# The sample group's HGRN step: v spread over the partitions by TensorE, state loaded on GpSimd's queue, each head placed behind the prompt's own

## The chip, the cores and the metric

The kernel runs on one core of one Trainium2 chip. The metric is the device time of one execution in microseconds, of which the median over several runs is given.

## What is computed

The kernel is one step of a one-layer decoder with two groups of heads: attention heads and four HGRN2 heads of width 128. It runs for a prompt of 1024 tokens and for 8 samples of one token each, with the same weights. The change touches the HGRN2 heads of the 8 samples. Each sample b and head h has a state S of 128 key rows by 128 value columns, loaded from `state_hgrn`. With one token the reference's step is (cut from `_hgrn_chunk` and `_hgrn_inputs`):

```python
f = lb + (1.0 - lb) * sigmoid(z['f_b'])
k = (1.0 - lb) * sigmoid(-z['f_b'])
q = silu(z['q_b'])
v = z['i_b']
S_new = f[:, None] * S + k[:, None] * v[None, :]
o = q @ S_new
```

`f`, `k` and `q` are one number for each key row, `v` is one for each value column. `S_new` is an output (`hgrn_state_sample`), and `o` goes on, normalised, into the layer's output. The prompt's HGRN heads do the same over 1024 tokens, in chunks.

## The kernel before

`project()` (L280) normalises x, multiplies it by the wide input weight and runs the HGRN heads. The projections are float32 products made of three single-pass products (`xhi`/`xlo` by `w_hi`/`w_lo`, accumulated in `pa`); `feat` makes columns of features, `tok` rows of tokens. Each weight block is loaded by SP (`w_raw<-w_in`), then split by ScalarE (`w_hi`) and VectorE (`w_lo`). These weight matmuls are most of TensorE's work in this part and fill the time in which the HGRN heads wait for other engines.

The prompt heads are `hgrn_a(h)` (within-chunk sums `AT`, on all engines) and `hgrn_b(h)` (the running state `S` and the output `O`). At the end of `hgrn_b`, VectorE makes the norm `o_rs`, GpSimd scales `O` by it (L605), TensorE transposes `O` in two halves (`pt<-ident,O`, L609), ScalarE copies each half to `ot` (one buffer) and SP stores it to `oT_d`.

The sample heads are the generator `hgrn_sample()` (L419); each step from one `yield` to the next does one head. `v` is in `vs`, 8 partitions by 512. Before, it is written to a DRAM tile `v_d` once; each head loads it back to all 128 partitions as `vb` (L436, 512 KB) and loads its state `S` (L434, 512 KB), both on SP. VectorE multiplies `vb` by `k` (L438), GpSimd multiplies `S` by `f` (L439), VectorE adds them (L440), SP stores the sum. Then the sum is split into `S0h` (ScalarE) and `S0l` (VectorE), and 16 small products with `qp` make `o` in the PSUM tile `pt`.

Buffers are shared by tag in the pool `hp`, two of each tag: `S0` with the prompt state `S`, `vb` with `O`, `S0h`/`S0l` with the forget gates `F`. PSUM has one buffer for `pt`, two for `ph`, three for `pa`.

The code's order is not the program's: a list scheduler orders the instructions of each engine by its own estimate of durations. An engine then runs its instructions strictly in that order. `go(n)` in `project()` advances the sample generator and so says where in the code a sample head stands. Before, heads 0 and 1 stand between `hgrn_a(3)` and `hgrn_b(3)`, head 2 and 3 behind that.

Of the kernel before, what the change touches and what calls it, by code (L numbers as in the profile page):

```python
# [7 lines left out]
F32 = mybir.dt.float32  # L8
# [5 lines left out]
OP = mybir.AluOpType  # L14
# [6 lines left out]
NB = 8  # L21
# [6 lines left out]
class Kernel:  # L28
# [251 lines left out]
    def project(self, ctx):  # L280
        nc, a = self.nc, self.a
# [36 lines left out]
        def ev_q(h0):  # L318
            def ev(f, ts, p):
                h = h0 + f  # L320
                if ts.start == 0:
                    Q[h] = hp.tile([128, TS], F32, name="Q")
                nc.scalar.activation(Q[h][:, ts], p, AF.Sigmoid)
                nc.vector.tensor_tensor(Q[h][:, ts], p, Q[h][:, ts], op=OP.mult)
            return ev
# [10 lines left out]
        self.page_index(self.cp)  # L336
        smp = self.hgrn_sample()
        next(smp)
        for h in range(2):
            self.hgrn_b(h, *st[h])  # L340
        self.feat((C_FB + 256, 2, ev_f(2)))
        self.feat((C_QB + 256, 2, ev_q(2)))
        go = lambda n: [next(smp, None) for _ in range(n)]
        for h in range(2, 4):
            st = self.hgrn_a(h, Q[h], K[h], F[h])
            go(2 if h == 3 else 0)
            self.hgrn_b(h, *st)
            go(1 if h == 3 else 0)

        def ev_z(dst, scale):  # L350
            def ev(f, ts, p):
# [67 lines left out]
    def hgrn_sample(self):  # L419

        nc, hp, a = self.nc, self.hp, self.a
        f, k, q = (self.sfkq[:, i] for i in range(3))
        v_d = self.dram.tile([NB, 512], F32, name="v_d")
        self.after(self.pidma, nc.sync.dma_start(v_d, self.vs))
        o = hp.tile([32, 128], F32, name="so", bufs=1)
        for h in range(4):
            yield
            po = self.ps_t.tile([128, 512], F32, name="pt")[:64, :128]
            qp = hp.tile([128, NB, 64], F32R, name="qp", bufs=1)
            nc.vector.tensor_scalar(qp.rearrange("p (a c) d -> p a (c d)", c=2), self.ones[:, None, :].to_broadcast([128, 4, 128]), 0.0, None, op0=OP.mult)  # L430
            qv = qp.rearrange("p b c -> p (b c)")
            self.split(qv[:, h * NB:h * NB + 456:65], qv[:, 32 + h * NB:32 + h * NB + 456:65], q[:, h], nc.vector, nc.vector)
            S = hp.tile([128, NB, 128], F32, name="S0", tag="S")
            nc.sync.dma_start(S, a["state_hgrn"][0, :, h].rearrange("b k v -> k b v"))  # L434
            vb = hp.tile([128, NB, 128], F32, name="vb", tag="O")
            nc.sync.dma_start(vb, bass.AP(tensor=v_d.tensor, offset=v_d.offset + h * 128, ap=[[0, 128], [512, NB], [1, 128]]))  # L436
            bc = lambda t: t[:, h, :, None].to_broadcast([128, NB, 128])
            nc.vector.tensor_tensor(vb, vb, bc(k), op=OP.mult)  # L438
            nc.gpsimd.tensor_tensor(S, S, bc(f), op=OP.mult)  # L439
            nc.vector.tensor_tensor(S, S, vb, op=OP.add)  # L440
            nc.sync.dma_start(a["hgrn_state_sample"][0, :, h].rearrange("b k v -> k b v"), S)
            hi = hp.tile([128, NB, 128], F32R, name="S0h", tag="F")
            lo = hp.tile([128, NB, 128], F32R, name="S0l", tag="F")
            self.split(hi, lo, S, nc.scalar, nc.vector)
            for b in range(NB):
                self.mm(po, qp[:, b], hi[:, b], b == 0, False)
                self.mm(po[:32], qp[:, b, :32], lo[:, b], False, b == NB - 1)
            if h:
                nc.vector.tensor_tensor(o, o, po[:32], op=OP.add)
            else:  # L450
                nc.vector.tensor_copy(o, po[:32])
            nc.vector.tensor_tensor(o, o, po[32:], op=OP.add)
        sq = hp.tile([32, 128], F32, name="ssq", bufs=1)
        ss = hp.tile([128, 1], F32, name="sr", bufs=1)[:32]
        nc.scalar.activation(sq, o, AF.Square, accum_out=ss)
        nc.vector.tensor_scalar(ss, ss, 1.0 / 128, EPS, op0=OP.mult, op1=OP.add)
        r = hp.tile([128, 1], F32, name="srs", bufs=1)[:32]
        self.rsqrt(hp, r, ss)
        nc.vector.tensor_scalar(o, o, r, None, op0=OP.mult)
        pt = self.ps_t.tile([128, 512], F32, name="pt")[:, :32]  # L460
        nc.tensor.transpose(pt, o, self.ident[:32, :32])
        oT = hp.tile([128, 32], F32, name="soT", bufs=1)
        nc.scalar.copy(oT, pt)
        nc.scalar.dma_start(self.oT_d[:, :, T:].rearrange("h v b -> v h b"), oT.rearrange("p (h b) -> p h b", b=NB))
# [177 lines left out]
    def page_index(self, pool):  # L642

        nc = self.nc
        pt = self.a["page_table"]
        raw = pool.tile([128, NB], I32, name="pt_raw", bufs=1)
        for i in range(8):
            dma = nc.sync.dma_start(raw[16 * i:16 * i + 16], bass.AP(tensor=pt.tensor, offset=pt.offset + i, ap=[[0, 16], [8, NB]]))
            if i == 0:
                self.pidma = dma  # L650
        lane = pool.tile([128, NB], I32, name="pt_lane", bufs=1)
        nc.gpsimd.iota(lane, pattern=[[0, NB]], base=0, channel_multiplier=1)
        nc.vector.tensor_scalar(lane, lane, 15, None, op0=OP.bitwise_and)
# [740 lines left out]
```

## Time and profile before

| | us |
|---|---|
| median of 3 runs | 1093.54 |
| lowest and highest | 1088.66, 1094.07 |
| the profiled execution | 1092.95 |
| its span in the trace | 1091.2 |
| TensorE busy (96%) | 1051.9 |
| VectorE busy (57%) | 618.0 |
| ScalarE busy (36%) | 388.5 |
| GpSimd busy (22%) | 241.1 |

The mean granted clock of TensorE is 0.984 of full speed. PE is TensorE, DVE VectorE, ACT ScalarE, POOL GpSimd; SP issues most DMAs. "Busy" of TensorE counts overlapping matmuls once, and a busy TensorE is not one at its peak. In a timeline the bracket behind a row tells how long its engine had been idle and what ended that. The HGRN part lies between about 80 and 390 us of the span, the sample heads between 282 and 376 us.

### The profile page before, as it was taken

Reading aid. Unit: us, or ns where it says so; the run is one execution under the profiler, and the core shown is the slowest. Engines: PE = TensorE matmul, PEld = TensorE weight load, DVE = VectorE, ACT = ScalarE, POOL = GpSimd, SP = SyncE. Lnnn points to the kernel's source line nnn. Section 1 sums busy time; section 2 is a strip of 40 time slices with the busy share of each in tenths; the row PEclk is TensorE's granted clock in tenths of the full one; section 3 lists DMA queues with packets and bytes.
Section 4 is the critical chain, followed back from the end, with each engine's and each line's share of the span. In section 5 each row is a group of like instructions: output and inputs, shape, how many; then the busy total and the mean of one; then the engine's idle time right before and its main releaser. Section 6 shows DMA issues by size and latency. Waiting matters only on the chain.

```text
span 1091.2 us, 18921 instructions
## 1 busy us (share of the span) xinstructions
PE 1051.9 (96%) x7021; PEld 936.8 (86%) x7021; DVE 618.0 (57%) x1822; ACT 388.5 (36%) x786; POOL 241.1 (22%) x276
## 2 busy tenths in 40 slices
PE   4999999999899899999989999999999999999998
PEld 3898799999789899999968898888788888778876
DVE  6847565666484535543574666766655677461223
ACT  4622234313133335432224544553554332241112
POOL 0024231331031133002023111111323133131111
PEclk9999999999999999999969999999999999999999
DMA  6212023333454666304468711001831474131110
GB/s 195 78 29 68 11 72 100 117 101 120 144 173 135 193 222 208 135 1 118 123 186 250 189 38 42 20 21 41 230 111 42 137 199 119 41 97 49 47 37 31
DMA packets 119007, 116.44 MB, mean 107 GB/s; under 512 B 18902, under 2 KB 101166, under 8 KB 116612
## 3 DMA queue, kind: packets, MB, share of 16 engines
q1 hardware_dynamic: 97412, 79.46, 25.6%
q10 hardware_dynamic: 19200, 19.01, 5.1%
q0 software_dynamic: 2304, 16.78, 4.6%
q8 instruction: 55, 0.90, 0.4%
q14 instruction: 36, 0.29, 0.1%
HBM read 84.84 MB, written 29.31 MB: 105 GB/s over the span
## 4 chain that ended last, share of the span: by engine, by line
PE 81%; DMA 9%; DVE 5%; issue 2%; ACT 1%; POOL 1%; SPq 0%; ACTq 0%; DVEq 0%; POOLq 0%
PE pa L42 37%; PE pb L42 27%; PE ph L42 9%; PE pt L42 4%; DMA vb<-v_d 2%; DMA w_raw<-w_in 2%; PE ph L714 1%; DMA w1r<-cmp_w 1%; DMA fw_raw<-w_out 1%; PE pa L1124 1%; DMA f_z<-oT_d 1%; DMA cg<-cache_cmp_kv,pidx 1%; DMA V<-x_prompt 1%; PE ph L1318 1%; DVE w_lo L239 1%
## 5 line engine op out<-in xcount | busy, mean ns | idle before, releaser
L42 PEld LDWEIGHTS pb<-V,P 128*128 128x128 f32 x1056 | 143.8, 194 | 11.8 <-POOL P L959 0.9
L42 PE MATMUL pb<-V,P 128*128 128x128 f32 x1056 | 149.2, 279 | 0.5 <-DVE mx L908 0.4
L42 PE MATMUL pa<-xhi,w_hi 128*128 128x344 f32 x384 | 125.7, 329 | 3.3 <-ACT w_hi L238 1.7
L42 PE MATMUL pa<-xlo,w_hi 128*128 128x344 f32 x384 | 124.2, 325 | 0.0
L42 PE MATMUL pa<-xhi,w_lo 128*128 128x344 f32 x384 | 123.3, 326 | 0.0
L954 ACT ACTIVATE P<-ph 128x512 f32<-128x512 f32 (+4 forms) x148 | 85.8, 595 | 100.4 <-PE ph L42 78.3
L915 DVE CUSTOM_DVE_ANT_0 junk<-pa,mask 128x320 bf16<-128x320 f32 (+5 forms) x150 | 73.1, 496 | 35.7 <-PE pa L42 35.1
L42 PE MATMUL pa<-w_lo,xhi 128*128 128x256 f32 (+2 forms) x256 | 79.8, 316 | 0.1
L42 PE MATMUL pa<-w_hi,xlo 128*128 128x256 f32 (+2 forms) x256 | 79.6, 315 | 0.0
L42 PE MATMUL pa<-w_hi,xhi 128*128 128x256 f32 (+2 forms) x256 | 78.9, 317 | 0.0
L42 PEld LDWEIGHTS pa<-xhi,w_hi 128*128 128x128 f32 x384 | 73.3, 191 | 5.0 <-ACT w_hi L238 2.4
L238 ACT ACTIVATE w_hi<-w_raw,gpre 128x512 fp32r<-128x512 f32 (+2 forms) x80 | 47.4, 616 | 78.1 <-DMA w_raw<-w_in 46.5
L42 PEld LDWEIGHTS pa<-xlo,w_hi 128*128 128x128 f32 x384 | 73.2, 191 | 0.1
L42 PEld LDWEIGHTS pa<-xhi,w_lo 128*128 128x128 f32 x384 | 72.7, 190 | 0.4 <-DVE w_lo L239 0.2
L42 PE MATMUL ph<-QA,KA 128*128 128x512 f32 (+4 forms) x148 | 66.4, 451 | 2.5 <-ACT P L954 2.5
L42 PE MATMUL pa<-KB,QB 65*128 65x320 f32 (+6 forms) x195 | 64.8, 369 | 1.1 <-DVE mx L915 0.7
L239 DVE SCALAR_TENSOR_TENSOR w_lo<-w_raw,gpre,w_hi 128x512 fp32r<-128x512 f32 (+2 forms) x80 | 51.4, 663 | 21.6 <-ACT w_hi L238 20.9
L42 PE MATMUL pa<-fw_hi,yh 128*128 128x512 f32 (+1 forms) x160 | 61.7, 385 | 0.0
L42 PE MATMUL pa<-fw_hi,yl 128*128 128x512 f32 (+1 forms) x160 | 61.6, 385 | 0.0
L42 PE MATMUL pa<-fw_lo,yh 128*128 128x512 f32 (+1 forms) x160 | 61.6, 385 | 0.0
L42 PE MATMUL ph<-QB,KB 68*128 68x512 f32 (+3 forms) x148 | 58.5, 405 | 0.0
L42 PE MATMUL pb<-x,w1h 128*128 128x384 f32 (+1 forms) x192 | 55.9, 353 | 0.3 <-ACT x L50 0.3
(457 smaller groups left out, 2391.3 us busy)
## 6 DMA issues: line engine op xcount, KB each, us to landing
w_raw<-w_in SPq DMA_DIRECT2D x32, 256.0 KB
w_raw<-w_in SPq DMA_DIRECT2D x48, 128.0 KB
VS<-sg SPq DMA_DIRECT2D x8, 512.0 KB
sg<-cache_win_kv SPq DMA_DIRECT2D x16, 256.0 KB
fw_raw<-w_out SPq DMA_DIRECT2D x16, 256.0 KB
fw_raw<-ple_gate SPq DMA_DIRECT2D x16, 256.0 KB
f_x<-x_prompt SPq DMA_DIRECT2D x8, 512.0 KB
win_kv_sample<-cache_win_kv SPq DMA_DIRECT2D x8, 511.0 KB
```

Source lines behind the costliest of these rows:

```text
L42: return self.nc.tensor.matmul(out, lhsT, rhs, start=start, stop=stop, skip_group_check=True)
L238: nc.scalar.activation(hi, raw, AF.Copy, scale=g)
L239: nc.vector.scalar_tensor_tensor(lo, raw, g, hi.bitcast(F32), op0=OP.mult, op1=OP.subtract)
L714: nc.tensor.transpose(pt[:, i * 128:(i + 1) * 128], src[b0 + j // 2, kv][:, j % 2, 2 * jp:2 * jp + 2].rearrange("p j d -> p (j d)"), self. ...
L915: nc.vector.tensor_tensor_reduce(junk, pm, mk, 1.0, -1e30, op0=OP.add, op1=OP.max, accum_out=o)
L954: nc.scalar.activation(P, ps, AF.Exp, scale=0.125)
L1124: nc.tensor.transpose(pt[:, j * 128:(j + 1) * 128], rows(j), self.ident)
L1318: nc.tensor.transpose(pt[:, c], h[:, k * 128:(k + 1) * 128], self.ident[:n, :n])
```

## The change

It has three parts. `v_d` and the four `vb` loads go; for each half of a head four fp32 products with a broadcast column of the identity (`self.ident[:NB, i + b]`, 8 partitions, as the stationary operand) put row b of `vs` on all 128 partitions in a PSUM tile `ph`, and VectorE multiplies by `k` from there. The state's load is issued by GpSimd and not by SP. And the generator is advanced earlier: heads 0 and 1 right behind the prompt's `hgrn_b(0)` and `hgrn_b(1)`, heads 2 and 3 each behind the prompt's own; the projection of `Q` for heads 2 and 3 now comes ahead of that of `F`. A manual order between two DMAs (`pidma`) goes with `v_d`.

```diff
@@ project
         smp = self.hgrn_sample()
         next(smp)
+        go = lambda n: [next(smp, None) for _ in range(n)]
         for h in range(2):
             self.hgrn_b(h, *st[h])
+        go(2)
+        self.feat((C_QB + 256, 2, ev_q(2)))
         self.feat((C_FB + 256, 2, ev_f(2)))
-        self.feat((C_QB + 256, 2, ev_q(2)))
-        go = lambda n: [next(smp, None) for _ in range(n)]
         for h in range(2, 4):
             st = self.hgrn_a(h, Q[h], K[h], F[h])
-            go(2 if h == 3 else 0)
             self.hgrn_b(h, *st)
-            go(1 if h == 3 else 0)
+            go(1)
@@ hgrn_sample
-        v_d = self.dram.tile([NB, 512], F32, name="v_d")
-        self.after(self.pidma, nc.sync.dma_start(v_d, self.vs))
...
-            nc.sync.dma_start(S, a["state_hgrn"][0, :, h].rearrange("b k v -> k b v"))
+            nc.gpsimd.dma_start(S, a["state_hgrn"][0, :, h].rearrange("b k v -> k b v"))
             vb = hp.tile([128, NB, 128], F32, name="vb", tag="O")
-            nc.sync.dma_start(vb, bass.AP(tensor=v_d.tensor, offset=v_d.offset + h * 128, ap=[[0, 128], [512, NB], [1, 128]]))
             bc = lambda t: t[:, h, :, None].to_broadcast([128, NB, 128])
-            nc.vector.tensor_tensor(vb, vb, bc(k), op=OP.mult)
+            for i in range(0, NB, 4):
+                pv = self.ps_h.tile([128, 512], F32, name="ph").rearrange("p (b v) -> p b v", b=4)
+                for b in range(4):
+                    self.mm(pv[:, b], self.ident[:NB, i + b:i + b + 1].to_broadcast([NB, 128]), self.vs[:, h * 128:h * 128 + 128], True, True)
+                nc.vector.tensor_tensor(vb[:, i:i + 4], pv, bc(k)[:, i:i + 4], op=OP.mult)
             nc.gpsimd.tensor_tensor(S, S, bc(f), op=OP.mult)
```

The scheduler orders every engine anew. Three places matter below. In TensorE's order before, from the two halves of prompt head 1's `O` on (`ident,O` are their transposes, `pa` are weight matmuls):

```order
L42 MATMUL pa<-xlo,w_hi 128x344
L609 MATMUL pt<-ident,O 128x128 x4
L42 MATMUL pa<-xhi,w_lo 128x344
...
L609 MATMUL pt<-ident,O 128x128 x4
L42 MATMUL pa<-xhi,w_lo 128x344
```

The same place after the change, from the last product of prompt head 1 (`ph<-S,Q`) to the next weight matmul behind the products with the sample states (`S0h`, `S0l`):

```order
L42 MATMUL ph<-S,Q 128x128
L42 MATMUL ph<-vs,ident 128x128 x12
L42 MATMUL pa<-xhi,w_hi 128x344
...
L42 MATMUL ph<-vs,ident 128x128 x4
...
L42 MATMUL pa<-xhi,w_lo 128x344
L610 MATMUL pt<-ident,O 128x128 x8
L42 MATMUL pt<-S0h,qp 64x128
L42 MATMUL pt<-S0l,qp 32x128
...
L42 MATMUL pa<-xhi,w_hi 128x344
```

Between the twelve and the four spread products stand 23 weight matmuls, behind them 49; then both halves of the transposes follow on each other, and on them the 32 products with the states of sample heads 0 and 1, with no weight matmul between. Before, 24 weight matmuls stood between the two halves.

On GpSimd's queue, from the scaling of prompt head 0's `O` to that of head 1's and the work on head 2 that follows (`sfkq` takes the samples' f, k, q; the state's product is L439 before and L440 after). Before:

```order
L605 TENSOR_TENSOR O<-O,o_rs 128x1024
L470 COPY sfkq<-F 128x8
L470 COPY sfkq<-K 128x8
L477 MEMSET AT 128x1024
L605 TENSOR_TENSOR O<-O,o_rs 128x1024
L470 COPY sfkq<-Q 128x8
L474 TENSOR_TENSOR QK<-Q,K 128x1024
```

After:

```order
L606 TENSOR_TENSOR O<-O,o_rs 128x1024
L432 DMA S_1702<-state_hgrn 128x8x128
L440 TENSOR_TENSOR S_1702<-S_1702,sfkq 128x1024
L478 MEMSET AT 128x1024
L432 DMA S_1747<-state_hgrn 128x8x128
L471 COPY sfkq<-Q 128x8
L440 TENSOR_TENSOR S_1747<-S_1747,sfkq 128x1024
L606 TENSOR_TENSOR O<-O,o_rs 128x1024
```

The loads and products of both sample heads now stand ahead of the scaling of prompt head 1's `O`.

On SP's queue before, where sample heads 0 and 1 stand among the weight loads:

```order
L233 DMA w_raw<-w_in 128x512 x3
L436 DMA vb<-v_d 128x8x128 x2
L434 DMA S_2555<-state_hgrn 128x8x128
L434 DMA S_2590<-state_hgrn 128x8x128
L441 DMA hgrn_state_sample<-S_2555 128x8x128
```

After the change, at prompt head 1:

```order
L583 DMA hgrn_state_prompt<-S 128x128
L233 DMA w_raw<-w_in 128x256
L442 DMA hgrn_state_sample<-S_1702 128x8x128
L442 DMA hgrn_state_sample<-S_1747 128x8x128
L613 DMA oT_d<-ot 128x512 x2
L233 DMA w_raw<-w_in 128x256 x4
```

The two stores of the sample states stand ahead of the two stores of prompt head 1's output; the loads of `vb` and `S` are no longer on this queue.

## Rows read from the trace of the kernel before

**Rows 1.** The page: TensorE's busy time, and the chain that ended last, by engine.

```profile
PE 1051.9 (96%) x7021; PEld 936.8 (86%) x7021; DVE 618.0 (57%) x1822; ACT 388.5 (36%) x786; POOL 241.1 (22%) x276
...
PE 81%; DMA 9%; DVE 5%; issue 2%; ACT 1%; POOL 1%; SPq 0%; ACTq 0%; DVEq 0%; POOLq 0%
```

**Rows 2.** TensorE by windows: stretch, its length, busy (instructions), granted clock, DMA share, GB/s.

```profile
280.00:290.00 10.00, 7.63 (x55) 1.00 0.30 81
290.00:300.00 10.00, 7.76 (x44) 0.83 0.60 178
300.00:310.00 10.00, 9.49 (x63) 0.83 0.56 164
310.00:320.00 10.00, 8.46 (x133) 1.00 0.47 137
...
360.00:370.00 10.00, 6.58 (x34) 0.83 0.46 153
```

**Rows 3.** Waits: who waited for what, us in total, times, longest.

```profile
DVE vb L438 <- DMA vb<-v_d: 16.6, 4, 5.1
```

**Rows 4.** Timeline of VectorE: start, us, engine, line, operation, [idle before <-releaser].

```profile
287.88 1.22 DVE L438 TENSOR_TENSOR vb<-vb,sfkq 128x1024 f32<-128x1024 f32 x1 [5.08 <-DMA vb<-v_d]
...
361.06 1.23 DVE L438 TENSOR_TENSOR vb<-vb,sfkq 128x1024 f32<-128x1024 f32 x1 [2.83 <-DMA vb<-v_d]
362.20 0.16 DVE L84 SCALAR_TENSOR_TENSOR o_rs<-rs_t,rs_g 128x8 f32<-128x8 f32 x1
362.37 1.23 DVE L440 TENSOR_TENSOR S<-S,vb 128x1024 f32<-128x1024 f32 x1
```

**Rows 5.** Timeline of TensorE at two matmuls that waited.

```profile
290.36 0.50 PE L42 MATMUL ph<-PQh,ones 128*128 128x512 f32 x1 [2.73 <-DVE AT L517]
...
365.41 0.65 PE L609 MATMUL pt<-ident,O 128*128 128x128 f32 x4 [3.42 <-POOL O L605]
```

**Rows 6.** Timeline of GpSimd: the scaling of O of prompt head 3.

```profile
362.50 2.85 POOL L605 TENSOR_TENSOR O<-O,o_rs 128x1024 f32<-128x1024 f32 x1 [5.50 <-DVE o_rs L84]
```

**Rows 7.** Chain of waits, 170 to 200 us: start, us, what, records.

```profile
180.30 1.78 PE ph L42 x16
182.09 10.68 PE pa L42 x68
```

**Rows 8.** Operations of L42: duration in ns (min/median/max), first and last start, shapes.

```profile
L42 PE MATMUL pb<-V,P x1056: 270/275/582, 565.2 to 863.1; 128*128 128x128 f32 x176
...
L42 PE MATMUL pb<-vc,P x128: 270/272/576, 560.0 to 854.8; 47*128 47x128 f32 x16, 55*128 55x128 f32 x16, 63*128 63x128 f32 x16, 39*128 39x128 f32 x16
```

**Rows 9.** Chain of waits, 275 to 380 us: sample head 1's 16 state products.

```profile
317.14 1.13 PE pt L42 x16
```

**Rows 10.** Timeline of VectorE: a small step, a copy from PSUM, a split.

```profile
186.15 0.17 DVE L82 TENSOR_TENSOR rs_t<-rs_g 128x8 f32<-128x8 f32 x1
...
306.84 0.73 DVE L537 COPY_PREDICATED AT<-lm,ph 128x512 f32<-128x512 uint8 x1
...
308.07 1.22 DVE L51 TENSOR_TENSOR S0l<-S,S0h 128x1024 fp32r<-128x1024 f32 x1
```

**Rows 11.** Timeline of ScalarE: both ot copies of prompt head 0, and S0h.

```profile
173.22 0.59 ACT L611 COPY ot<-pt 128x512 f32<-128x512 f32 x1
...
177.31 0.59 ACT L611 COPY ot<-pt 128x512 f32<-128x512 f32 x1 [0.30 <-DMA oT_d<-ot]
...
303.00 1.04 ACT L50 CAST S0h<-S 128x1024 fp32r<-128x1024 f32 x1 [0.93 <-DVE S L440]
```

**Rows 12.** Timeline of SP: the state load of sample head 2.

```profile
328.91 0.38 SPq L434 DMA_DIRECT2D S<-state_hgrn  x1
```

**Rows 13.** Timeline of GpSimd: its product with that state.

```profile
333.43 1.90 POOL L439 TENSOR_TENSOR S<-S,sfkq 128x1024 f32<-128x1024 f32 x1 [4.75 <-DMA S<-state_hgrn]
```

**Rows 14.** Tile cg: GpSimd's indirect loads of 1 MB, issue in ns, and landing.

```profile
L659 POOL DMA_INDIRECT cg<-cache_cmp_kv,pidx x8: 936/945/1167, 394.0 to 454.5; - x8
...
DMA to landing us min/median/max: 5.4/7.7/9.0
```

More of the change, by code (lines that the diff above doesn't have):

```diff
@@ L647, in page_index @@
         for i in range(8):
-            dma = nc.sync.dma_start(raw[16 * i:16 * i + 16], bass.AP(tensor=pt.tensor, offset=pt.offset + i, ap=[[0, 16], [8, NB]]))
-            if i == 0:
-                self.pidma = dma
+            nc.sync.dma_start(raw[16 * i:16 * i + 16], bass.AP(tensor=pt.tensor, offset=pt.offset + i, ap=[[0, 16], [8, NB]]))
         lane = pool.tile([128, NB], I32, name="pt_lane", bufs=1)
```

## The prediction

> **What bounds the kernel now.** I read the page first: TensorE is busy 96% of the span, and the chain that ended last is 81% TensorE [rows 1]. So a change is worth what TensorE idles less, less what it must do more. The busy time by stretch (windows of 10 us) then shows where it idles while the sample's HGRN step runs [rows 2]: busy 7.63, 7.76, 9.49 and 8.46 of 10 us from 280 to 320, and 6.58 from 360 to 370. That is 2.37 + 2.24 + 0.51 + 1.54 + 3.42 = **10.1 us of idle**. Three of these windows also show a granted clock of 0.83, that is a part of them at the lower level, 1.2 GHz, right after TensorE had stood idle. Each costs up to 0.17 x 10 = 1.7 us, together **5.1 us**. The two sums make **15.2 us**, all that this step loses on the path.
>
> The waits name the cause: VectorE waited 16.6 us in four pieces for the broadcast copy `vb<-v_d` [rows 3]. The timeline shows how this gets to TensorE. VectorE sat 5.08 us before the product at 287.88, and a matmul that needed the `AT` copy queued behind it waited 2.73 us at 290.36 [rows 4, 5]. At 361.06 it sat 2.83 us; behind it stood `o_rs` at 362.20, which GpSimd's scaling of `O` awaited (5.50 us idle, then 2.85 us of work), and TensorE's transposes of `O` started 3.42 us late [rows 4 to 6].
>
> **Removed.** The store of `v_d` and the four `vb` loads leave SP; VectorE no longer waits for them. I take all 15.2 us as gone, **-15.2**. The lower end is 13.7: the 1.54 us between 310 and 320 had been released by other work of VectorE and may stay.
>
> **Added on TensorE.** Each head needs 8 fp32 products of 128x128, 32 in all. The nearest rows are the prompt heads' own 128x128 fp32 products: a piece of the chain of 16 records takes 1.78 us, two records to a product, so 0.222 us each [rows 7]. 32 x 0.222 = **+7.1 us**, on an engine with no room. Only 8 partitions are contracted, but 47 instead of 128 saved nothing elsewhere (medians 272 and 275 ns) [rows 8]. The lower end is that of the sample's single-pass products, 16 in 1.13 us [rows 9]: 32 x 0.071 = 2.3. VectorE now multiplies 8 times from PSUM, at about the 0.73 us of the copy from PSUM, and not 4 times at 1.22 [rows 4, 10]: +1.0 us, hidden beside weight matmuls; without that cover it would be a wait of TensorE for a PSUM buffer (third rival).
>
> **Moved: heads 0 and 1, place A.** Time zero is the end of prompt head 1's last `S,Q` product. TensorE then does 16 spread products (3.6 us) and 72 weight matmuls at 10.68/68 = 0.157 us [rows 7] (11.3 us), and waits about 0.5 us for a PSUM buffer that ScalarE's copy (0.59 us, [rows 11]) frees. It reaches `O`'s transposes at 15.4. These need a chain which now contains the sample head. The prompt state must be stored before its buffer can be loaded (3.5 us, as the store of `ot`, copied by 173.81 and landed by 177.31 [rows 11]), and it is ready at 0.3, so GpSimd issues the state load at 3.8. That load took 4.5 us on SP (328.91 to 333.43) [rows 12, 13]; no row shows a plain load on GpSimd's queue. Its indirect loads of twice the bytes landed in 5.4 to 9.0 us, median 7.7 [rows 14]. I take 5.5, nearest to SP's row, which has the same pattern and size, plus a microsecond for GpSimd's 0.94 us of issue. Then multiply 1.90, add 1.23, five small operations of `o_rs` at 0.2, scaling as long as the multiply (same shape) [rows 4, 10, 13]: 3.8 + 5.5 + 1.9 + 1.2 + 1.0 + 1.9 = 15.3. That is just in time, so **no wait here**; every microsecond over 5.6 is one of TensorE.
>
> One rule speaks against the new queue. By the Trainium skill's "SBUF — State Buffer", section "SBUF: two separate sides", a DMA issued by GpSimd is held up while VectorE runs operations that lock the port they share. Its example is 620 ns alone and 3,100 ns beside a copy; an estimate by that page makes the load 2.5 us longer and the sum that much larger. No run here shows it yet.
>
> Then comes what the new order itself costs. Both transposes of `O`, both products with the state and the casts between them stand back to back on TensorE, with no weight matmul between, over one `pt` buffer and one `ot` buffer. TensorE waits for ScalarE's first copy, 0.6. The second copy must wait until the first store has landed, 3.5 after the first copy: 3.5 - 0.4 (the second transposes) + 0.6 = 3.7. Head 1's `S0h` and `S0l` take the buffers of head 0's, so their casts, 1.04 and 1.22 [rows 10, 11], run only after head 0's products: 2.3. The first sigmoid of the next projection waits for the same buffers, 0.6. Sum 7.2 us of idle, and one window at the lower clock, 1.7: **+8.9**. Lower end 3.5 (no wait for the store, no slow clock).
>
> **Moved: head 2 and head 3, places B and C.** Here the state buffer is free early, and between the last product and the transposes lie 66 and 68 weight matmuls, 8 to 10 us, with more weight matmuls between the transposes and the state products. The chain behind them (product, add, five small steps, scaling) is 6 to 7 us. I take **0**; the upper end is the stall of before, 3.4 us [rows 5].
>
> The state loads leave SP's queue, where the weights' loads stand; and the projections of `Q` and `F` change places, which moves sigmoids but adds no work. I cost both at nothing: weight matmuls cover them.
>
> **Sum.** The profiled execution took 1092.95 us; 1092.95 - 15.2 + 7.1 + 8.9 + 0 = 1093.75. The median of the runs is 0.6 higher, so **1094.4 us** against 1093.54. A measurement can tell about 0.5%, 5.5 us, from no change, so this is "no change". Its own range: 8.9 down to 3.5 gives 1089.0, 3.4 at B or C gives 1097.8.
>
> **Rivals.**
> *Faster: the old waits go and little comes instead (33%).* If the first half's store lands while the other wait runs and the clock stays up, place A costs only the 2.3 us of casts: 1094.4 - 6.6 = **1087.8**; with nothing at all there, 1085.5. For it: earlier stores of `ot` cost TensorE nothing, since its transposes lay apart. Against: now they do not.
>
> *Slower: GpSimd's queue delivers the state late (20%).* Its indirect load describes 128 rows and keeps GpSimd 0.94 us [rows 14]; the state load has 1,024 runs of 512 bytes. If issue goes by runs, it takes 8 x 0.94 = 7.6 us, and with SP's 4.5 the load lands 12.1 after it is issued, 6.5 over the point of 5.6 from which it decides. GpSimd is held, `O`'s scaling is late, TensorE waits at place A; with one more window at the lower clock: 1094.4 + 6.5 + 1.7 = **1102.6**. The indirect loads' 9.0 would give 3.4 + 1.7, 1099.5. For it: the load's chain lies in front of the transposes with a tenth of a microsecond to spare. Against: nothing in the profile ties issue to runs. The page named above would add to it: what starves is the writing of descriptors.
>
> *The wait only changes its name (7%).* The first twelve spread products need three `ph` buffers of two, so TensorE itself waits for VectorE's multiplies. If each of the eight is waited for, 8 x 0.73 = 5.8: **1100.2**. Against: the other halves stand apart, between weight matmuls.
>
> **How the numbers follow.** Forecast 40% (1089.0 to 1097.8), faster rival 33%, slower rivals 27%. Under 1088.1 is faster, over 1099.0 slower: 0.33, 0.40, 0.27. The range must take both sides in: from just under "nothing new at place A" (1085) to the late state load (1103).
>
> **What the profile after would show.** Right: no VectorE wait on a DMA for `vb`; windows full at the places of 280 to 310 and 360 to 370 of before; 32 new `ph<-vs,ident` products of two records each, about 0.22 us apart; and, right after head 1, a stretch of some 10 us in which TensorE is busy 3 to 4 us, first behind ScalarE's `ot` copy (released by the DMA `oT_d<-ot`), then behind `S0l`. Wrong, to the fast side: that stretch is nearly full. Wrong, to the slow side: GpSimd's multiply of the state waits on its load longer than 5.6 us after issue, or TensorE waits at `pt<-ident,O` for GpSimd's `O`; or the spread products cost clearly more or less than 7 us.

## The result and the profile after

| us | before | after |
|---|---|---|
| median (6 runs each) | 1093.61 | 1125.25 |
| lowest and highest | 1088.66, 1094.08 | 1120.82, 1126.65 |
| the profiled execution | 1092.95 | 1120.82 |
| its span | 1091.2 | 1119.1 |

The ratio is 1.0288 [1.0259, 1.0316]: the change makes the kernel **slower by 2.9%**, outside the predicted range. The profiled execution is the fastest of the runs after, so what follows explains the 27.9 us between the two spans, not the 31.6 between the medians.

The page after, busy time and the chain that ended last. They answer to [rows 1]:

```profile
PE 1065.4 (95%) x7085; PEld 946.6 (85%) x7085; DVE 620.4 (55%) x1826; ACT 388.3 (35%) x786; POOL 245.9 (22%) x280
...
PE 85%; DMA 8%; DVE 4%; issue 1%; ACT 1%; SPq 0%; ACTq 0%; DVEq 0%
```

TensorE's busy time grew by 13.5 us with 64 more matmul records, and the span by twice that. TensorE by windows after (stretch, its length, busy, granted clock, DMA share, GB/s): the place of prompt head 1 (A), the stretch that answers to [rows 2], and the place of the last spread products:

```profile
180.00:190.00 10.00, 6.38 (x53) 1.00 0.72 219
190.00:200.00 10.00, 10.00 (x56) 0.83 0.40 116
200.00:210.00 10.00, 7.23 (x51) 0.90 0.29 90
210.00:220.00 10.00, 7.11 (x39) 0.50 0.04 16
220.00:230.00 10.00, 10.00 (x61) 0.92 0.01 2
230.00:240.00 10.00, 7.84 (x58) 1.00 0.48 151
...
280.00:290.00 10.00, 10.00 (x87) 1.00 0.18 61
290.00:300.00 10.00, 10.00 (x84) 1.00 0.41 132
300.00:310.00 10.00, 9.06 (x71) 1.00 0.48 140
310.00:320.00 10.00, 8.68 (x76) 1.00 0.45 134
...
380.00:390.00 10.00, 10.00 (x68) 1.00 0.22 75
```

Where before lost 15.2 us [rows 2] the windows are nearly full, at the full clock: 2.3 us idle are left between 300 and 320, and none at the last head. Before, the same stretch was full at the full clock:

```profile
180.00:190.00 10.00, 10.00 (x70) 1.00 0.28 87
190.00:200.00 10.00, 10.00 (x68) 1.00 0.14 54
200.00:210.00 10.00, 10.00 (x77) 1.00 0.49 157
210.00:220.00 10.00, 9.90 (x80) 1.00 0.46 146
```

After, place A is idle for 3.62 + 2.77 + 2.89 + 2.16 = 11.4 us. Its clock falls, to a mean of 0.50 in one window: that window ran at 1.2 GHz throughout. Time lost to the clock, as (1 - granted clock) times busy time, is 1.7 + 0.7 + 3.6 + 0.8 = 6.8 us.

A finer account takes the time from each matmul's start to the next one's start and subtracts what that kind of matmul takes at the full clock; what is left is called **lost time** here. It is worked out from TensorE's whole timeline, so it contains both idle time and slow clock:

| lost time of TensorE, us | before | after |
|---|---|---|
| 0 to 40 (start) | 8.5 | 13.3 |
| to 240 (place A in it) | 4.0 | 23.8 |
| to the last product with a sample state | 18.9 | 6.9 |
| from there to the attention's first V,P product | 16.3 | 17.1 |
| attention | 30.3 | 32.8 |
| finish | 4.1 | 9.0 |
| sum | 82.1 | 102.9 |

The sum grew by 20.8, and the work itself, at the full clock, by 7.2. Together they are the span's 27.9 (28.0 with rounding).

**Place A, wait by wait.** Every row of TensorE's timeline between 180 and 240 with an idle time in front of it (the bracket gives it, and what ended it):

```profile
183.51 0.49 PE L42 MATMUL ph<-V,AT 128*128 128x128 f32 x2 [1.57 <-ACT O L598]
188.69 2.05 PE L42 MATMUL ph<-vs,ident 8*128 8x128 f32 x16 [2.05 <-ACT O L598]
206.18 0.66 PE L610 MATMUL pt<-ident,O 128*128 128x128 f32 x4 [0.68 <-ACT ot L612]
208.93 0.37 PE L42 MATMUL pt<-S0h,qp 128*64 128x128 f32 x1 [2.09 <-ACT ot L612]
212.30 0.34 PE L42 MATMUL pt<-S0h,qp 128*64 128x128 f32 x1 [1.40 <-DVE qp L51]
213.34 0.31 PE L42 MATMUL pt<-S0l,qp 128*32 128x128 f32 x1 [0.70 <-DVE S0l L51]
215.93 0.66 PE L42 MATMUL pa<-xhi,w_hi 128*128 128x344 f32 x1 [0.79 <-ACT K L312]
232.89 0.39 PE L42 MATMUL pa<-w_lo,xhi 128*128 128x256 f32 x1 [1.49 <-DVE w_lo L239]
235.56 0.51 PE L42 MATMUL pa<-w_hi,xhi 128*128 128x256 f32 x2 [0.67 <-ACT w_hi L238]
```

They fall into three kinds. The first two (3.6 us) wait for ScalarE's copy of `O` out of the PSUM tile `ph`. The next five (5.7 us) are the block that the prediction described: both transposes, both heads' state products, one `pt` buffer, one `ot` buffer, the casts in between. One part of it the prediction did not name: the 1.40 us end with `qp`, which has a single buffer too and is filled for head 1 only after head 0's products. The last two (2.2 us) wait for weights. Their sum is the 11.4 us of the windows.

Why the `O` copies are late stands on ScalarE's timeline, with the `ot` copies, of which the second had to wait for the first one's store:

```profile
187.66 0.51 ACT L238 ACTIVATE w_hi<-w_raw,gpre 128x256 fp32r<-128x256 f32 x1 [2.89 <-DMA w_raw<-w_in]
188.08 0.56 ACT L598 COPY O<-ph 128x512 f32<-128x512 f32 x1
...
205.54 0.58 ACT L612 COPY ot<-pt 128x512 f32<-128x512 f32 x1 [11.99 <-PE pt L610]
208.29 0.58 ACT L612 COPY ot<-pt 128x512 f32<-128x512 f32 x1 [2.16 <-DMA oT_d<-ot]
```

The copy itself had nothing more to wait for; it stood behind `w_hi`, which waited 2.89 us for a block of weights.

**GpSimd's queue.** The state's loads after, and GpSimd's timeline at place A:

```profile
L432 POOL DMA_DIRECT2D S<-state_hgrn x4: 922/940/1155, 171.8 to 360.5; - x4
...
DMA to landing us min/median/max: 4.6/4.7/4.7
```

```profile
189.14 0.95 POOL L432 DMA_DIRECT2D S<-state_hgrn  x1 [2.78 <-DVE w_lo L239]
...
193.86 2.78 POOL L440 TENSOR_TENSOR S<-S,sfkq 128x1024 f32<-128x1024 f32 x1 [3.05 <-DMA S<-state_hgrn]
200.24 1.90 POOL L606 TENSOR_TENSOR O<-O,o_rs 128x1024 f32<-128x1024 f32 x1 [3.60 <-DVE o_rs L84]
```

Issue takes 0.94 us and landing 4.6 to 4.7, against 4.5 on SP [rows 12, 13]. The profile has the landing of two of the four loads; the multiplies that waited for the four started 4.7 to 5.1 us after the issues. `O` was scaled by 202.1, 2.8 us before TensorE reached its transposes at 204.90.

**The start.** Before the sample step is reached, the kernel is already late: TensorE's first wait of note after, then VectorE's row that held it up:

```profile
30.10 1.11 PE L218 MATMUL ph<-ident,V 128*128 128x128 f32 x4 [8.13 <-DVE rs_g L80]
```

```profile
28.22 0.17 DVE L654 SCALAR_TENSOR_TENSOR pidx<-pt_raw,pt_lane 128x8 int32<-128x8 int32 x1 [8.20 <-DMA w_raw<-w_in]
```

The bracket names a weight load, but `pidx` reads none: it is made of the eight page-table loads `pt_raw`, and a wait is put down to whatever landed last. SP's timeline of before and of after at the same place:

```profile
16.97 3.27 SPq L648 DMA_DIRECT2D pt_raw<-page_table  x7
```

```profile
16.85 3.75 SPq L649 DMA_DIRECT2D pt_raw<-page_table  x8
```

Before, the manual order held one of the eight loads back behind the store of `v_d` (it was issued at 140.2), and `pidx`, which needs all eight, stood at 144.2 on VectorE. Without that order all eight go out at 17, and the scheduler puts `pidx` 164 rows earlier on VectorE. There it sits for 8.2 us, and the norms and the splitting of the weights stand behind it. The first transposes of `K` start at 149.0 and not at 144.0.

### The profile page after: what moved, and what is told of

It reads as the page before. It is cut to its first block, busy times and chain, and to the rows that moved or that the text cites. A ratio compares the mean times of both kernels' runs of the same rounds, so it can differ in the third digit from the quotient of the medians.

```text
span 1119.1 us, 19019 instructions
## 1 busy us (share of the span) xinstructions
PE 1065.4 (95%) x7085; PEld 946.6 (85%) x7085; DVE 620.4 (55%) x1826; ACT 388.3 (35%) x786; POOL 245.9 (22%) x280
## 4 chain that ended last, share of the span: by engine, by line
PE 85%; DMA 8%; DVE 4%; issue 1%; ACT 1%; SPq 0%; ACTq 0%; DVEq 0%
PE pa L42 40%; PE pb L42 27%; PE ph L42 9%; PE pt L42 4%; DMA fw_raw<-w_out 2%; DMA w_raw<-w_in 2%; PE ph L713 1%; DMA fw_raw<-ple_gate 1%; DMA x_in<-x_prompt 1%; PE pa L1123 1%; DMA oT_d<-ot 1%; DVE fw_lo L51 1%; PE ph L1317 1%; PE ph L218 1%; ACT fw_hi L50 0%
## 5 line engine op out<-in xcount | busy, mean ns | idle before, releaser
L42 PEld LDWEIGHTS pb<-V,P 128*128 128x128 f32 x1056 | 144.7, 194 | 13.2 <-POOL P L958 0.9
L42 PE MATMUL pb<-V,P 128*128 128x128 f32 x1056 | 150.5, 279 | 0.6 <-DVE mx L907 0.4
L42 PE MATMUL pa<-xhi,w_hi 128*128 128x344 f32 x384 | 127.5, 334 | 2.4 <-ACT xhi L50 1.0
L42 PE MATMUL pa<-xlo,w_hi 128*128 128x344 f32 x384 | 125.0, 328 | 0.0
L42 PE MATMUL pa<-xhi,w_lo 128*128 128x344 f32 x384 | 123.4, 327 | 0.0
L42 PE MATMUL pa<-w_lo,xhi 128*128 128x256 f32 (+2 forms) x256 | 79.6, 314 | 2.4 <-DVE w_lo L239 2.4
L42 PE MATMUL pa<-w_hi,xhi 128*128 128x256 f32 (+2 forms) x256 | 78.0, 314 | 2.0 <-ACT G L371 1.3
L42 PE MATMUL pa<-w_hi,xlo 128*128 128x256 f32 (+2 forms) x256 | 79.3, 313 | 0.0
L42 PEld LDWEIGHTS pa<-xhi,w_hi 128*128 128x128 f32 x384 | 74.3, 194 | 4.1 <-ACT xhi L50 1.4
L42 PEld LDWEIGHTS pa<-xlo,w_hi 128*128 128x128 f32 x384 | 74.3, 194 | 0.1
L42 PEld LDWEIGHTS pa<-xhi,w_lo 128*128 128x128 f32 x384 | 73.7, 193 | 0.4
L42 PE MATMUL ph<-QA,KA 128*128 128x512 f32 (+4 forms) x148 | 67.2, 456 | 3.7 <-ACT P L953 3.5
L42 PE MATMUL pa<-KB,QB 65*128 65x320 f32 (+6 forms) x195 | 64.6, 367 | 1.5 <-DVE mx L914 0.7
L42 PE MATMUL pa<-fw_hi,yh 128*128 128x512 f32 (+1 forms) x160 | 62.4, 390 | 2.3 <-ACT fw_hi L50 2.2
L42 PE MATMUL pa<-fw_lo,yh 128*128 128x512 f32 (+1 forms) x160 | 62.0, 388 | 0.4 <-DVE fw_lo L51 0.4
L42 PE MATMUL pa<-fw_hi,yl 128*128 128x512 f32 (+1 forms) x160 | 61.8, 386 | 0.0
L557 POOL TENSOR_TENSOR K<-K,E 128x512 f32<-128x512 f32 x24 | 35.2, 1468 | 113.1 <-PE pb L42 51.6
L42 PE MATMUL ph<-QB,KB 68*128 68x512 f32 (+4 forms) x148 | 58.9, 407 | 0.0
```

Of the source, the lines that this page charges most:

```text
L42: return self.nc.tensor.matmul(out, lhsT, rhs, start=start, stop=stop, skip_group_check=True)
L557: nc.gpsimd.tensor_tensor(Kv[:, :, 0], Kv[:, :, 0], Ev[:, :, 1:2].to_broadcast([128, nb, m]), op=OP.mult)
```

## The experiments

They ran in four sessions, each on a chip of its own, with before beside them. Before had medians there of 1095.4 to 1096.2, by which each ratio is taken; 95% intervals in brackets. The theory: the manual order's removal costs the start, the placement costs place A, the spread costs its own 7 us, GpSimd's queue costs nothing. "Placement" means here both that the heads move and that the projections of Q and F change places; the two were not tried apart. The main rivals: the spread products or the queue cause what place A shows.

**The manual order alone.** Before, without it:

```diff
-        self.after(self.pidma, nc.sync.dma_start(v_d, self.vs))
+        nc.sync.dma_start(v_d, self.vs)
```

> The kernel before with one line less: the manual order that held the first page-table load back until after the store of v_d (pidma). All else as before. My theory: with it gone all eight page-table loads stand early on SP's queue, VectorE's index arithmetic pidx moves to the front of VectorE's order (row 80 instead of row 244) and blocks VectorE until these loads have landed, as in the changed kernel, where VectorE sat 8.2 us before pidx and TensorE 8.1 us before the transposes behind it. Expected: 5.0 us longer than before (1098 to 1099), the first transpose of K (ph<-ident,K) 4 to 6 us later than 144.0, the HGRN part and the rest as before within 2 us. Rival: the 5 us of the changed kernel's start come from the weights' loads landing later, not from pidx; then this kernel is within 1.5 us of before.

1103.61 (5 runs), ratio 1.0072 [1.0033, 1.0111]. The first transposes of `K` start at 149.2, lost time to 40 us is 13.6, and the row that did it is there:

```profile
28.24 0.17 DVE L655 SCALAR_TENSOR_TENSOR pidx<-pt_raw,pt_lane 128x8 int32<-128x8 int32 x1 [7.94 <-DMA w_raw<-w_in]
```

That line alone costs some 8 us by the medians, of which 5.1 lie in the start. The expectation had 5.0 in all; where the other 3 lie is open.

**After, with the manual order back.** The store of `v_d` comes back too, though nothing reads it:

```diff
+        v_d = self.dram.tile([NB, 512], F32, name="v_d")
+        self.after(self.pidma, nc.sync.dma_start(v_d, self.vs))
...
+            if i == 0:
+                self.pidma = dma
```

> The changed kernel with the manual order put back: a store of v_d that nothing reads (16 KB) and the first page-table load held behind it. Theory (the order costs 5 us): 1125.2 - 5.0 = 1120, start as in the kernel before (first ph<-ident,K near 144). If the removed order were also what moved the attention and the output stage (2.3 and 5.2 us longer in the changed kernel), 1112 to 1113. Rival (loads landing late): within 1.5 us of 1125.

1116.3 (4 runs), ratio 1.0186 [1.0144, 1.0229]. The start is that of before (8.5 us lost, `K` at 143.8). The whole is 4 us under the expected 1120. What remains is 20.6 us over before, and place A is as it was: 23.3 us lost from `K`'s transposes to 240. (Its profiled execution is the slowest of its four, so its whole span, 1119.4, says less than the median.)

**The state's load back on SP**, in the kernel above:

```diff
-            nc.gpsimd.dma_start(S, a["state_hgrn"][0, :, h].rearrange("b k v -> k b v"))
+            nc.sync.dma_start(S, a["state_hgrn"][0, :, h].rearrange("b k v -> k b v"))
```

> As the run with the manual order put back, but the sample state's load issued by SP as before. Theory: GpSimd's queue is not what costs; its loads landed 4.6 to 4.7 us after issue in the changed kernel, as SP's 4.5 did, so within 3 us of the run with the order alone (1117 to 1123). Rival (GpSimd's queue delivers late and blocks GpSimd): 5 us or more faster than it.

1116.64 (4 runs), 1.0202 [1.016, 1.0244]; 22.8 us lost at place A. The queue makes no difference that four runs can tell.

**The old placement**, spread and queue as after, manual order kept:

```diff
-        go(2)
-        self.feat((C_QB + 256, 2, ev_q(2)))
         self.feat((C_FB + 256, 2, ev_f(2)))
+        self.feat((C_QB + 256, 2, ev_q(2)))
...
+            go(2 if h == 3 else 0)
             self.hgrn_b(h, *st)
-            go(1)
+            go(1 if h == 3 else 0)
```

> As the run with the manual order put back, but the four sample heads where they stood before (heads 0 and 1 between hgrn_a(3) and hgrn_b(3), heads 2 and 3 behind it) and the projection of F ahead of Q again; spread by TensorE and state load by GpSimd stay. Theory: the placement is the main cost (two O transposes and 32 state products back to back behind prompt head 1, and weight loads stuck behind the stores on SP). Then this is about 1093.5 - 15.2 + 7.1 = 1085, at most 1093. Rival (the spread on TensorE is what costs): 1105 or more.

1094.97 (10 runs), 1.0 [0.9972, 1.0027]: 21.3 us faster than with the new placement. Lost time from `K`'s transposes to 240 is that of before (2.3 against 2.4). So placement is what costs place A; but the level is 10 us over the expectation. The old waits are gone here as well (6.7 us lost from 240 to the last state product, 18.9 before), and 7.2 of those 12 go to the spread. (The profiled execution is the slowest of its ten.) Of the rest one part shows on TensorE's timeline; the work of the next stage now comes earlier than its load:

```profile
390.13 0.22 PE L672 MATMUL pt<-ident,pe_t 32*128 32x32 f32 x1 [2.92 <-DMA pe_t<-cmp_pe]
```

In before this matmul starts at 400.1 and does not wait. Another part shows in the granted clock; the run with the spread alone, below, has it too.

**The new placement alone**, with the `vb` loads, SP's queue and the manual order of before:

```diff
+        go(2)
+        self.feat((C_QB + 256, 2, ev_q(2)))
         self.feat((C_FB + 256, 2, ev_f(2)))
-        self.feat((C_QB + 256, 2, ev_q(2)))
...
-            go(2 if h == 3 else 0)
             self.hgrn_b(h, *st)
-            go(1 if h == 3 else 0)
+            go(1)
```

> The kernel before with the new placement alone: heads 0 and 1 behind hgrn_b(0) and hgrn_b(1), heads 2 and 3 each behind the prompt's own, Q projected ahead of F. v still goes through v_d and vb, the state is loaded by SP, the manual order stays. Theory: the placement by itself costs, by the back-to-back products behind prompt head 1, the slow clock after them and the weights' loads held up on SP; TensorE's lost time there (20 us between 160 and 240 in the changed kernel) stays mostly, and the vb waits come on top: 1108 to 1120. Rival: the placement costs only together with the spread on TensorE, whose products need the PSUM buffers that ScalarE's copies of O free; then within 5 us of before (1091 to 1101).

1108.21 (4 runs), 1.0141 [1.008, 1.0201]. Place A loses 23.2 us here without a single spread product. The largest wait is that of the block, since `ot`'s store stood behind a state store on SP, and the clock follows:

```profile
202.84 0.37 PE L42 MATMUL pt<-S0h,qp 128*64 128x128 f32 x1 [5.68 <-ACT ot L611]
```

```profile
200.00:210.00 10.00, 4.27 (x33) 0.50 0.24 80
```

The old waits go here too, though `vb` is still loaded. VectorE still waits for it,

```profile
DVE vb L438 <- DMA vb<-v_d: 8.8, 3, 4.5
```

but TensorE is idle for only 1.8 us between 280 and 340, at the full clock. So either part of the change, the placement or the spread, takes most of the old waits off the path; together they do not gain twice.

**The spread alone**, at the old place, with SP's queue:

```diff
-            nc.vector.tensor_tensor(vb, vb, bc(k), op=OP.mult)
+            for i in range(0, NB, 4):
+                pv = self.ps_h.tile([128, 512], F32, name="ph").rearrange("p (b v) -> p b v", b=4)
...
+                nc.vector.tensor_tensor(vb[:, i:i + 4], pv, bc(k)[:, i:i + 4], op=OP.mult)
```

> The kernel before with the spread by TensorE alone: old placement, state load by SP, manual order kept (the store of v_d stays, unread). Theory (GpSimd's queue is neutral, the spread takes the vb waits away for 7.1 us of products): within 3 us of the run that also loads by GpSimd (1095.0). Rival (GpSimd's queue costs or helps): 4 us or more away from it, either side.

1094.81 (10 runs), 0.9995 [0.997, 1.0019], the same as with GpSimd's queue. Spreading by TensorE instead of the DMA is worth nothing on the whole: what the waits give is spent on the products, on the clock and on what is late next. The clock falls twice here although TensorE is not idle once between 243 and 387:

```profile
300.00:310.00 10.00, 10.00 (x134) 0.83 0.62 172
...
340.00:350.00 10.00, 10.00 (x59) 0.84 0.38 114
```

Both falls come about 1 us behind sixteen spread records in a row, which started at 299.70 and 343.91 and ran for 2 us. They cost 1.7 + 1.6 = 3.3 us. The old placement with GpSimd's queue shows the same two, at 302 and 346. The prediction had not priced this: beside its 7.2 us the spread costs, at the old place, about half of that again in clock.

**Three attempts to mend place A.** First, the spread products in the PSUM tile `pb` and not in `ph`, so that they need not wait for the `O` copy:

```diff
-                pv = self.ps_h.tile([128, 512], F32, name="ph").rearrange("p (b v) -> p b v", b=4)
+                pv = self.ps_b.tile([128, 512], F32, name="pb").rearrange("p (b v) -> p b v", b=4)
```

> The changed kernel with the manual order back, and the spread products in the PSUM buffers of pb instead of ph. Theory: the 1.57 and 2.05 us that TensorE waited at 183.51 and 188.69 for ScalarE's copy of O (itself behind a w_hi that waited for its weights) fall away at the second place, and with them part of the slow clock: 3 to 6 us under the run with the order alone (1116.3), 1110 to 1113. Rival (the wait only moves to the next product that needs a buffer): within 1.5 us of it.

1113.73 (4 runs), 1.0147 [1.0083, 1.0211], inside the interval of the kernel that it changes. The waits for the `O` copy are gone, but new ones stand in their place. TensorE now arrives at the transposes earlier, and waits there for GpSimd, which waited for `o_rs`; that stood on VectorE behind a `w_lo` that had waited 4.02 us for its weights.

```profile
194.91 2.75 POOL L608 TENSOR_TENSOR O<-O,o_rs 128x1024 f32<-128x1024 f32 x1 [1.91 <-DVE o_rs L84]
...
197.71 0.65 PE L612 MATMUL pt<-ident,O 128*128 128x128 f32 x4 [1.74 <-POOL O L608]
```

A wait for weights later on grew from 1.42 to 2.87 us. Idle time from 170 to 240 falls from 11.9 to 10.3 us, and lost time at A from 23.3 to some 19, with the products counted at 0.11 us a record as in `ph`. A miss of the 3 to 6 us expected, and a useful one: this wait alone was not the bound.

Second, the block itself: the state products go to `pb` and no longer share the one `pt` buffer with the transposes.

```diff
-            po = self.ps_t.tile([128, 512], F32, name="pt")[:64, :128]
+            po = self.ps_b.tile([128, 512], F32, name="pb")[:64, :128]
```

> The changed kernel with the manual order back, and the 16 products with the sample state in the PSUM buffers of pb instead of the one of pt. In TensorE's order the products then no longer follow the two O transposes without a weight matmul between; the transposes lie 18 weight matmuls and more apart. Theory (the chain over the one pt buffer, and the 1.2 GHz stretch that its idle brings, is most of what the new place costs): lost time of TensorE up to the last state product falls from 30.7 to about 18 us, the whole from 1116.3 to 1104 to 1108. Rival (the place costs by the weights' loads on SP, stuck behind the sample states' stores and the O copies behind w_hi): less than 4 us under 1116.3.

1110.2 (6 runs), 1.0132 [1.0102, 1.0162]; lost time at A falls from 23.3 to 13.6. The scheduler now spreads transposes and state products between weight matmuls, and TensorE's windows from 200 on are nearly full, at the full clock. What is left stands ahead of them:

```profile
170.00:180.00 10.00, 7.96 (x63) 1.00 0.66 194
180.00:190.00 10.00, 7.80 (x41) 0.73 0.58 179
190.00:200.00 10.00, 10.00 (x70) 0.93 0.29 80
200.00:210.00 10.00, 9.61 (x74) 1.00 0.14 52
```

```profile
178.94 0.49 PE L42 MATMUL ph<-V,AT 128*128 128x128 f32 x2 [2.04 <-ACT O L600]
...
184.28 3.47 PE L42 MATMUL ph<-vs,ident 8*128 8x128 f32 x16 [2.20 <-ACT O L600]
```

Both are waits for the `O` copy. Of 9.7 us won at A, 6.1 arrive at the end, 2 fewer than the least that was expected.

Third, on top of that, the `O` copy by VectorE, past ScalarE's wait for weights:

```diff
-            nc.scalar.copy(O[:, 4 * g:4 * g + 4], po)
+            nc.vector.tensor_copy(O[:, 4 * g:4 * g + 4], po)
```

> As the run with the manual order and the state products in pb (1110.2), and the copies of O from PSUM made by VectorE instead of ScalarE, in every prompt head. Theory: the 2.04 and 2.20 us that TensorE still waited behind prompt head 1 (at 178.94 and 184.28 in that run) are ScalarE's: its copy of O stands behind a w_hi that waits for its weights; with another engine copying, both waits and the slow stretch after them shrink, lost time up to 240 falls from 13.6 to 8 or 9 us, the whole to 1104 to 1107. Rival: VectorE is held by the same weights (its w_lo stands behind w_hi), so the waits stay within 1 us of that and the whole within 2 us of 1110.

1108.17 (4 runs), 1.0112 [1.0074, 1.0151]. Lost time at A falls to 9.5, where 8 or 9 was expected, and the second wait is gone. The first has only changed its engine, for VectorE too stands behind split weights:

```profile
179.22 0.49 PE L42 MATMUL ph<-V,AT 128*128 128x128 f32 x2 [2.51 <-DVE O L600]
```

The whole gained 2.0 us, about what the rival had, which the two intervals don't tell apart from nothing.

**A cheaper spread.** At the old place: `v` is kept as two single-pass parts, on partitions 0 to 7 and 32 to 39, and a column that selects both makes one single-pass product out of each fp32 product:

```diff
-        vs = hp.tile([NB, 512], F32, name="vs", bufs=1)
+        vs = hp.tile([40, 512], F32R, name="vs", bufs=1)
...
+                nc.vector.tensor_tensor(vs[32:40], p, vs[:NB].bitcast(F32), op=OP.subtract)
...
+        nc.vector.tensor_tensor(sel, self.ident[:40, :NB], self.ident[:40, 32:40], op=OP.add)
...
```

> As the run with the manual order and the old placement (1095.0), but the spread in one pass: v is split once into high and low parts on partitions 0 to 7 and 32 to 39, and one float32r product with a selecting column adds both. Theory (the 32 products are wholly on the path, 0.222 us each in fp32 and about 0.06 in one pass): 32 x 0.16 = 5.2 us less, 1089 to 1091. Rival (they lie in time that TensorE waits anyway): within 1.5 us of 1095.

1090.27 (10 runs), 0.9956 [0.9933, 0.998]: **the fastest kernel of the study, 0.4% ahead of before.** 4.7 us under the same kernel with fp32 products. The products have 32 records and not 64, as far apart as those (0.11 to 0.12 us and not the 0.06 of the expectation), so about 3.6 us less work. And the two falls of the clock do not occur:

```profile
300.00:310.00 10.00, 10.00 (x143) 1.00 0.53 151
...
340.00:350.00 10.00, 10.00 (x64) 1.00 0.52 150
```

Against these gains the first transposes of `K` start 2.5 us later, at 146.3, for a reason that was not looked for.

**The two combined.** The cheaper spread and `pb` for the state products, at the new place:

```diff
-            po = self.ps_t.tile([128, 512], F32, name="pt")[:64, :128]
+            po = self.ps_b.tile([128, 512], F32, name="pb")[:64, :128]
...
+                    self.mm(pv[:, b], sel[:, i + b:i + b + 1].to_broadcast([40, 128]), self.vs[:, h * 128:h * 128 + 128], True, True)
```

> As the run before in this list, with the spread in one float32r pass. Theory: the pass saves 5 us here as it did at the old place (1095.0 to 1090.3), so 5 us under that run, 1099 to 1103. If the new place costs nothing once its products are apart, 1090.

1099.33 (12 runs), 1.0036 [1.001, 1.0063]: 10.9 us under the second attempt, over twice what the single-pass products gave at the old place. The clock (0.73 there) is 0.83 from 180 to 190 here, and the wait of the spread products for the `O` copy is gone; at the `V,AT` product before them a wait of 2.05 us stays, ended here by VectorE. The new placement is still behind the old one.

The same two at the old place:

```diff
-            po = self.ps_t.tile([128, 512], F32, name="pt")[:64, :128]
+            po = self.ps_b.tile([128, 512], F32, name="pb")[:64, :128]
```

> The old placement with the manual order, the one-pass spread, GpSimd's load, and the state products in pb: the candidate to beat both kernels. Theory (at the old place the pt buffer hardly holds TensorE back; its lost time there was 8.9 to 12.3 us up to the last state product, most of it from before the sample heads): within 2 us of the one-pass run, 1088 to 1092. Rival (pt is a bound there too): 1085 to 1087.

1093.01 (12 runs), 0.9977 [0.9959, 0.9996]; 1 us over what was expected at most, and no better than the cheaper spread alone. Where the block was never back to back, taking it apart brings nothing.

## Why the prediction was wrong, point by point

**The removed manual order, priced at nothing: wrong by 4.8 us in the profile.** The front of this document says that `pidma` goes with `v_d`, and the prediction has no sentence on it. Its removal takes away no work and no wait; it moves an instruction forward, to where its data is 8 us late, and VectorE runs what stands behind it only afterwards. The first experiment shows this alone, the second shows it undone.

**Place A, +8.9 predicted, 19.8 found (lost time to 240, 23.8 against 4.0).** The mechanism was right: transposes, casts and state products back to back, one buffer each, TensorE idle, the clock down. Its size was not. By the waits and windows above, which name 18.3 of the 19.8:

| term at place A | predicted | found |
|---|---|---|
| the block: `ot`'s store, casts, sigmoid | 7.2 | 5.7 |
| slow clock | 1.7 | 6.8 |
| `O` copy, PSUM tile `ph` | 0 | 3.6 |
| weights late | 0 | 2.2 |

The prediction knew of the `O` copy: it put 0.5 us for it into the time at which TensorE reaches the transposes, and left it out of the sum. It took the copy for as long as it runs, 0.59 us, not for when it can start, behind a `w_hi` that waits for its load. Of the block's four terms three came out within 0.2 us (0.7, 2.1 and 0.8 against 0.6, 2.3 and 0.6), the 2.1 in part through `qp`, which the prediction did not have; the store of `ot` held TensorE for 2.1 and not 3.7. And it gave one window of slow clock to 7 us of idle time. In [rows 2] three windows followed 10 us of idle time, at 1.7 each; here there are two stretches, the second with a whole window at 0.50. That the five waits of the block cause the second one was tried: with the block taken apart, the windows from 200 to 210 and 210 to 220 show 1.00. The first stretch starts at 191, behind a wait of 2.05 us and sixteen spread records; which of the two brings it was not tried. Why the weights come late at place A stays open. Q's weights are loaded ahead of F's there, and the DMA share is 0.72 between 180 and 190, but neither was tried by itself.

One zero in that sum came out by luck. TensorE was to reach the transposes 15.4 us after time zero and find `O` ready at 15.3. `O` was ready at 16.6 (202.1, counted from 185.5), and TensorE did not wait because the `O` copy and the slow clock had held it until 19.4. Where the copy no longer held it, in the first attempt to mend place A, it did wait, 1.74 us.

**The removed waits, -15.2 predicted, -12.0 found.** The four waits for `vb` are gone from the trace, as predicted. 6.9 us are still lost between 240 and the last state product. Among it are waits at 301 for VectorE's `w_lo` (0.94 us) and at 312 for ScalarE's `G` (1.32 us). Places B and C, priced at 0, are in this difference. The spread is not needed for this gain: the placement alone takes most of these waits off the path as well.

**The spread, +7.1 predicted, +7.2 found.** 64 records instead of none, 270 ns each at the median and 0.11 us apart, two to a product. What the prediction put at nothing is the clock that falls behind them, 3.3 us at the old place; at the new one only the first stretch of slow clock at A can be of that kind.

```profile
L42 PE MATMUL ph<-vs,ident x64: 270/270/371, 185.5 to 385.9; 8*128 8x128 f32 x64
```

**GpSimd's queue, 0 predicted, 0 found**, in the profile by multiplies that started 4.7 to 5.1 us after the issue where 5.6 was the point of decision, and by the two experiments with the load on SP (1116.64 against 1116.3 at the new place, 1094.81 against 1094.97 at the old one). The rival that made issue go by runs is refuted: 0.94 us for 1,024 runs, as for the 128 rows of the indirect load. The prediction weighed against it the Trainium skill's "SBUF — State Buffer", section "SBUF: two separate sides". The trace does not bear out its estimate of 2.5 us more: the two landings on record took 4.6 and 4.7. VectorE was idle during the first of the four issues and busy during the others; whether with operations of the kind that the section means was not tried. One load in the run with the products in `pb` took 7.8, with GpSimd held for the usual 0.95 us and the DMA share at 1.0 and more from 186 to 190.

**The other rivals.** That the wait would move to the `ph` buffers was given 7%, for VectorE's multiplies; the wait came, but for ScalarE's copy of `O`, which holds the same buffers. The faster rival needed the block to cost 2.3.

**What no term covered.** Attention lost 2.5 us more and the finish 4.9 (9.0 against 4.1). The last 2,492 matmuls of TensorE and 145 DMAs of SP follow in the same order in both traces, and over all profiles here the finish loses between 4.1 and 9.0. The 4.9 are therefore not put down to the change; their cause is open.

By the profile: spread 7.2, start 4.8, place A 19.8, old waits -12.0, from there to the attention 0.8, attention 2.5, finish 4.9: 28.0, against 27.9 between the spans. Without the three terms that were missing (start, `O` copy, weights) and with the slow clock as predicted, the change would still have cost 27.9 - 4.8 - 3.6 - 2.2 - 5.1 = 12.2 us, where the forecast had 0.8. So no single term makes the miss; most of these 12.2 are the attention and the finish (7.4) and the 3.2 us by which the old waits gave less.

## What to carry to other kernels

A removed ordering edge is part of the change, even with no work in it: look up in the new order of each engine which instructions moved forward, and ask for each when its data lands. Price a step that is moved onto the busiest engine's path by when its inputs and buffers can be ready, behind whatever else stands on the engines that make them, not by how long they run; idle time there was paid again in clock, and so, in two runs, was a row of sixteen products with few partitions. And when a wait goes, find what the next stage waits for before booking the gain: here 12 us of removed waits ended as nothing, until the replacement's own work was halved.

## What the runs showed of the hardware

- An fp32 product with 8 contracted partitions takes the records of one with 128: 270 ns each at the median, against 275 [rows 8]. Single-pass, it is one record and not two, at the same distance; by the whole kernel 32 of them saved 4.7 us.
- The granted clock fell with TensorE busy throughout: in both runs with the fp32 spread at the old place, twice, 0.83 or 0.84 over 10 us, each time shortly behind sixteen records with 8 contracted partitions. With the single-pass spread it stayed at 1.00 there. That the records cause it is argued from these three profiles, not tried by itself.
- A plain load of 512 KB with 1,024 runs kept GpSimd 0.94 us and landed in 4.6 to 4.7 us in the kernel after, while the same load took 4.5 on SP [rows 12, 13]. Over all kernels here that load it by GpSimd, landing took 4.6 to 7.8.
- Idle time need not lie in one piece to cost the clock: at place A five waits of 0.7 to 2.1 us, 5.7 us in all, lay between 205 and 216, with busy pieces of up to 2 us in between. By windows of 1 us the clock was 1.00 up to 208, within the second of these waits, and 0.52 in the next; from 210 to 220 it was 0.50, that is 1.2 GHz. The weight matmuls from 215.93 on were 0.29 us apart, and 0.16 from 221.78 on.
